# An encoder layer on one Trainium2 core: weight units of the head made one by one, and three output multiplications placed ahead of the last row tiles

## The chip, the cores and the metric

The kernel runs on one core of a Trainium2 chip. Its engines run side by side, each through its own list in order: TensorE (PE, with its weight loads shown as PEld), VectorE (DVE), ScalarE (ACT), GpSimd (POOL, which here issues transfers that add while they store) and SyncE (SP, which issues the plain transfers). They wait for one another through semaphores. The metric is the device time of one execution in microseconds; for the kernel before there are three runs and one profiled execution.

## The reference

One inference step of one layer of a hybrid streaming encoder, over 576 tokens (512 of a new stream, 64 of a running one) with 1024 features, all in fp32:

```
x += 0.5 * SwiGLU_1(RMSNorm(x))              # 1024 -> 2 * 2816 -> 1024
h  = RMSNorm(x); p = h @ w_in                # 7168 columns
y_a = (B * dwconv3(C * V)) @ w_a_out
y_b = swish(LN(dwconv31(GLU(U)) + bias)) @ w_b_out
x += (sigmoid(g_a) * y_a + sigmoid(g_b) * y_b) @ w_out
x += 0.5 * SwiGLU_2(RMSNorm(x))
y  = RMSNorm(x)
```

SwiGLU(v) is (silu(v @ W_gate) * (v @ W_up)) @ W_down. The outputs are y and the new histories of the two convolutions. Only the first SwiGLU (the head of the kernel) and the second one's last part with the final norm (its end) matter here.

## The kernel before

**Layout.** Features lie on the 128 partitions and tokens on the free axis, so an activation is 8 tiles of 128 x 576, and a product takes weights as the stationary operand and two halves of 288 tokens as the moving one.

**fp32 by parts.** Each fp32 operand v is cut into a high part hi (v rounded to the fp32r type, a copy on ACT) and a low part lo = v − hi, and a product is the sum of three matmuls: hi·hi, hi·lo, lo·hi. Weights are cut on the chip, in *units* of up to 512 columns. `Stream` (L195) keeps their order: SP loads raw weights into six buffers (`load`, L224), `add` (L246) makes sums of raws on DVE where a unit needs one, `begin` (L257) casts the high part on ACT, and `end` (L273) makes the low part on DVE. A unit of the kind "dma" has its low part made in another way: ACT also writes −hi, and a POOL transfer adds the raw to it (L267, L268). High and low parts live in tiles of two names, `g` and `u`, taken in turn, so that eight units are in flight at most. A raw buffer is loaded anew when the last unit that reads it is made.

**Lookahead.** `get(n)` (L298) gives unit n to a product. It first calls `lead(n)` (L287), which ends units up to n + ahead − 1, adds the sums of those up to n + ahead + 1 and begins those up to n + ahead. All this is decided while the program is built: the place of a call in the Python code is the place of its instructions in each engine's list.

**The head.** The first SwiGLU has 22 column tiles of gate and up weights, in four groups; the first group has tiles 0 to 4. Tiles 0 and 1 (all but the up weights of tile 1) are multiplied while x is still being loaded. Tiles 0 to 3 are `plain` (L738): a gate product, an up product, then on DVE and ACT `gate` (times the root of the norm, Silu), `hidden` (times up, high part) and `parts` (low part). From tile 4 on, `pair` (L777) computes gate and up of a tile by seven products in place of eight (a form of Strassen's method): sums and differences of weight blocks (s1 to s4) and of activation blocks. The units of the plan (L366 to L368) are, in order: 0 and 1 for up of tile 1, 2 and 3 for gate of tile 2, 4 and 5 for its up, 6 to 9 for tile 3, 10 to 16 for the seven products of tile 4 (10, 14 and 16 are of the kind "dma"; 11, 13 and 15 take the sums s2, s3 and s4, unit 12 takes s1, which is made when unit 10 is added), and from 17 on the down weights of the first group.

**The forms.** The activation side of the seven products needs four forms (`Forms`, L558), one for each pair of feature tiles p and p + 4: `scale` (two ACT operations), `combine` (four DVE operations of 288 columns, two high parts on ACT), `split` (two low parts on DVE). These steps are handed to the first `ffn` as a list, `todo` (L863 to L869), of which `forming` (L772) takes one entry at a time. A plain tile calls it after `gate` and after `parts`.

**The block of units.** After tile 0, `plain` calls `lead` for units 2 and 3, and after tile 1 for units 4 and 5 (L768 to L770), with a lookahead of six (L719).

**The end.** The last group of the second SwiGLU gives the eight row tiles of the output. Rows 3 to 7 (`LATE`) are computed in two passes, first for tokens 0 to 303 and then for tokens 304 to 575 (`LATE_SPANS`). After the first pass the squares of its tokens are summed (`gather`); in the second pass `put` (L1159) makes the root for the first span and returns four steps, each of which multiplies two row tiles by it on DVE and sends them out through SP. They are taken one after each row from row 4 on (L1187 to L1197). Each row of the second pass is taken up by DVE (L1184), squared on ACT, and the square added on DVE; the last square goes to PE by itself, and the root and the four multiplications of the second span close the kernel (L1200).

Of the kernel before, what the change touches and what calls it, by code (L numbers as in the profile page):

```python
# [42 lines left out]
LATE = range(3, KT)  # L43
# [17 lines left out]
AHEAD_UNITS = 6  # L61
# [45 lines left out]
def tile_encoder_step(  # L107
# [87 lines left out]
    class Stream:  # L195
# [88 lines left out]
            self.begin()  # L284
            self.end(low)

        def lead(self, n):  # L287

            self.load_ahead()
            n, total = n + self.ahead, len(self.units)  # L290
            while self.done < min(total, self.begun, n):
                self.end()
            while self.added < min(total, n + 2):
                self.add()
            while self.begun < min(total, n + 1):
                self.begin()
# [7 lines left out]
    ws = Stream(AHEAD_UNITS)  # L304
# [411 lines left out]
    name = ("f1", "u", 1)  # L716
    ps = product(name, xg)
    early[name] = ps
    ws.ahead = AHEAD_UNITS  # L719


    def update(j, ps, R=None):

# [8 lines left out]
    def ffn(f, xg, sums, finish, forms, R=None, todo=()):  # L732
        todo = list(todo)

        rest = []


        def plain(i, hs):  # L738
            nonlocal R
            t, up = ttile(), (f, "u", i)  # L740
            ps = product((f, "g", i), xg, order=IN_TURN if f == "f2" and i == 0 else None)
            got = None if up in early else chunks(up)
            if R is None:
                R = rstd(sums)
            ups = product(up, xg, got=got)
            hs.append(None)
            at = len(hs) - 1

            def gate():
                dve.tensor_tensor(halves(t), ps, halves(R), op=ALU.mult)  # L750
                sca.activation(t, t, AF.Silu)

            def hidden():
                dve.tensor_tensor(halves(t), ups, halves(t), op=ALU.mult)
                hs[at] = high(t)

            def parts():
                hs[at] = hs[at], low(t, hs[at])

            if f == "f2":  # L760
                rest.extend((gate, hidden, parts))
                return
            gate()
            forming()
            hidden()
            parts()
            forming()
            if i < 2:  # L768
                for n in plan[f, "gu"[i], 2]:
                    ws.lead(n)  # L770

        def forming():  # L772
            if todo:
                for step, p in todo.pop(0):
                    step(p)

        def pair(i, hs, last):  # L777
            qu, uu, t, cu = (ttile() for _ in range(4))
            q1, u2, u3, u4 = half(qu, 0), half(qu, 1), half(uu, 0), half(uu, 1)
            q = []  # L780

            def q7():
                dve.tensor_tensor(u3, q[3], u2, op=ALU.add)
                dve.tensor_tensor(half(cu, 1), u3, q[2], op=ALU.subtract)

            def gate():
                dve.tensor_tensor(half(t, 1), q[5], u4, op=ALU.add)
                dve.tensor_tensor(t, t, R, op=ALU.mult)
                sca.activation(t, t, AF.Silu)

            steps = (
                lambda: sca.copy(q1, q[0]),
                lambda: dve.tensor_tensor(u2, q[1], q1, op=ALU.subtract),
                lambda: dve.tensor_tensor(u4, q[2], u2, op=ALU.subtract),
                q7,
                lambda: dve.tensor_tensor(half(t, 0), q[4], q1, op=ALU.add),
                gate,
            )
            for n, xs in enumerate(bs):
                w = ws.get(plan[f, "s", i][n])  # L800
                q.append(bank()[:, :H])
                for k in range(KU):
                    (whi, wlo), (xh, xl) = w, xs[k]
                    for m, (l, r) in enumerate(((whi, xh), (whi, xl), (wlo, xh))):
                        pe.matmul(
                            q[n], l[:, k, :], r, start=k == m == 0, stop=k == KU - 1 and m == 2
                        )
                if n > 0:
                    steps[n - 1]()
                if rest:  # L810
                    rest.pop(0)()

            hs.append(None)
            at = len(hs) - 1

            def up():
                if last:
                    dve.tensor_tensor(t, t, R, op=ALU.mult)
                dve.tensor_tensor(half(cu, 0), q[6], u3, op=ALU.add)

            def hidden():
                dve.tensor_tensor(cu, cu, t, op=ALU.mult)
                hs[at] = high(cu)

            def parts():
                hs[at] = hs[at], low(cu, hs[at])

            rest.extend((up, hidden, parts))

        for g, grp in enumerate(GROUPS):  # L830
            hs = []
            for i in grp:
                if i < PLAIN[f]:
                    plain(i, hs)
                    continue
                if i == PLAIN[f]:
                    bs = forms.operands(xg)
                pair(i, hs, grp[-1] == FT - 1)
            while rest:
                rest.pop(0)()  # L840
            spare.clear()
            if grp[-1] < FT - 1:
                for j, ps in enumerate(both([(f, "d", g, j) for j in range(2)], hs)):
                    update(j, ps, R)
                for j in range(2, KT):
                    update(j, product((f, "d", g, j), hs), R)
            else:
                finish(g, hs)

    def finish1(g, hs):  # L850
        table(AF.Abs_reciprocal_sqrt)
        ps = both([("f1", "d", g, j) for j in range(2)], hs)
        for j in range(KT):
# [2 lines left out]
            nss.square(X[j])  # L856
            nss.add(dve)

    nss, nxg = Sum(), []
    one = forms1  # L860
    ffn(
        "f1", xg, ss, finish1, one, R1,
        (  # L863
            ((lambda _: ws.end(), None), (one.combine, 0), (one.scale, 1)),
            ((one.split, 0), (one.combine, 1), (one.scale, 2)),
            ((one.split, 1), (one.combine, 2), (one.scale, 3)),
            ((one.split, 2), (one.combine, 3)),
            ((one.split, 3),),
        ),  # L869
    )  # L870
    ss, xg = nss, nxg
# [266 lines left out]
    def finish2(g, hs):  # L1138
        fsum = Sum()
        table(AF.Abs_reciprocal_sqrt)  # L1140
        ps = both([("f2", "d", g, j) for j in range(2)], hs)
        for j in range(LATE[0]):
            update(j, ps[j] if j < 2 else product(("f2", "d", g, j), hs))
            fsum.square(X[j])
            fsum.add(dve)
        late = {}
        ydst = y.rearrange("(q a p) t -> q p a t", a=2, p=P)

        ys = {}

        def gained(j, span):

            n = span.stop - span.start
            q, a = j // 2, j % 2
            if a == 0:
                ys[q] = gtile(n=2 * n).rearrange("p (a n) -> p a n", a=2)
            sca.activation(ys[q][:, a, :], X[j][:, span], AF.Copy, scale=par(j, R_NF))

        def put(spans, ys, queues):  # L1159

            i, e = spans[0]
            RF = rstd(fsum, spans)[:, i:e].unsqueeze(1).broadcast_to((P, 2, e - i))

            def rows(q, v):
                dve.tensor_tensor(v, v, RF, op=ALU.mult)
                queues[q % 2].dma_start(ydst[q, :, :, i:e], v)

            return [(lambda q=q, v=v: rows(q, v)) for q, v in ys.items()]

        puts = []  # L1170

        for n, spans in enumerate(LATE_SPANS):
            i, e = spans[0]
            span = slice(i, e)
            fsum.n = LATE[0]
            done = dict(ys)
            for j in LATE:
                if n == 0:
                    late[j] = chunks(("f2", "d", g, j))
                ps = psum2()  # L1180
                for k, (w, kk) in enumerate(late[j]):
                    mm(ps, w, kk, hs[k], k == 0, k == len(hs) - 1, spans)
                xj = X[j][:, span]
                dve.scalar_tensor_tensor(  # L1184
                    xj, ps[:, 0, : e - i], 0.5, xj, op0=ALU.mult, op1=ALU.add
                )
                if n > 0 and j == LATE[1]:  # L1187
                    puts = put(LATE_SPANS[n - 1], done, (nc.sync, nc.sync))
                    fsum.terms = None
                fsum.square(X[j], span=span)  # L1190
                fsum.add(dve)
                if j == LATE[0]:
                    for b in range(LATE[0]):
                        gained(b, span)
                gained(j, span)
                if puts:
                    puts.pop(0)()  # L1197
            if n == 0:
                fsum.gather(span)
        for rows in put(spans, ys, (nc.sync, sca)):  # L1200
            rows()
# [47 lines left out]
```

## Time and profile before

| | |
|---|---|
| runs | 1306.09 us median of 3 (1305.59 to 1307.37) |
| profiled execution | 1304.71 us |
| its span, first to last instruction | 1302.9 us |
| mean granted PE clock | 0.996 |
| busy: PE, DVE, ACT, POOL | 99%, 68%, 59%, 29% of the span |
| PE's waits: for ACT's g tile, for a DMA into g | 3.7 us, 2.2 us |

In the profile nearly every instruction has line 83, that of a helper that records all operations, so operations are told apart by engine, tile names and shapes: `g<-raw` and `u<-raw` are high parts (ACT CAST), scalings by −1 (ACT ACTIVATE `g<-g`) or the adding transfers (POOL DMA) of weight units; `w<-raw,raw` and `w<-w,raw` are sums; `u<-w,u` and `g<-raw,g` low parts; `tmp<-w` and `tmp<-w,tmp` are `combine`, `act<-tmp` high parts and `act<-tmp,act` low parts of activations; `tmp<-mm,r` is a gate and `tmp<-mm,tmp` a product with up. All times are microseconds from the start of the span.

### The profile page before, as it was taken

How to read it: one execution, taken by the hardware profiler on the slowest of the kernel's cores; microseconds unless marked ns; L12 is line 12 of the kernel's file. 1: busy time of each engine (PE TensorE's matmuls, PEld its weight loads, DVE VectorE, ACT ScalarE, POOL GpSimd, SP SyncE). 2: the span in 40 equal slices, each digit the busy share in tenths (PEclk: the TensorE clock that was granted, in tenths of full speed). 3: DMA queues.
4: the chain of work that ended last, by engine and by line, in shares of the span. 5: the costliest groups of instructions: out<-in, count | busy, mean ns of one | idle time of the engine just before them, and what ended most of it. 6: DMA issues, size and time to landing. Idle time of an engine off the chain costs nothing.

```text
span 1302.9 us, 25690 instructions
## 1 busy us (share of the span) xinstructions
PE 1285.8 (99%) x9754; PEld 1283.6 (99%) x9754; DVE 892.3 (68%) x1469; ACT 768.5 (59%) x1362; POOL 380.7 (29%) x481
## 2 busy tenths in 40 slices
PE   9899999999999999999999999999999999999996
PEld 9899999999999999999999999999999999999996
DVE  6748758748945899888885260336967848847955
ACT  7555646645677654555544674457665655654664
POOL 0042332331242554333321322222142141241230
PEclk9999999999999999999999999999999999999998
DMA  7298796796798798878785978776687696796784
GB/s 220 61 175 181 142 196 146 163 194 148 161 185 184 163 214 174 169 168 177 172 169 124 200 160 175 160 163 145 138 169 176 147 195 155 157 210 136 158 176 106
DMA packets 287516, 215.39 MB, mean 165 GB/s; under 512 B 15520, under 2 KB 250016, under 8 KB 287392
## 3 DMA queue, kind: packets, MB, share of 16 engines
q0 software_dynamic: 59184, 97.28, 45.6%
q1 hardware_dynamic: 226336, 115.49, 31.2%
q8 instruction: 77, 1.26, 0.4%
q10 hardware_dynamic: 1872, 0.97, 0.3%
q14 instruction: 47, 0.39, 0.1%
HBM read 113.81 MB, written 2.62 MB: 89 GB/s over the span
## 4 chain that ended last, share of the span: by engine, by line
PE 94%; issue 2%; DVE 1%; ACT 1%; DMA 1%; POOL 0%; DVEq 0%; POOLq 0%; ACTq 0%
PE mm L83 94%; DVE tmp L83 1%; DMA g<-raw 0%; DMA raw<-in_ffn_w_gate_up_dram 0%; DVE g L83 0%; ACT w L83 0%; DMA act<-raw 0%; DVE x L83 0%; ACT act L83 0%; DVE act L83 0%; ACT tmp L83 0%; ACT r L83 0%; ACT L83 0%; DVEq L1239 0%; DVE u L83 0%
## 5 line engine op out<-in xcount | busy, mean ns | idle before, releaser
L83 PE MATMUL mm<-act,u 128*128 128x288 f32 x4686 | 659.9, 293 | 0.0
L83 PEld LDWEIGHTS mm<-act,u 128*128 128x128 f32 x4686 | 630.5, 188 | 0.0
L83 PE MATMUL mm<-act,g 128*128 128x288 f32 x2778 | 401.0, 295 | 5.9 <-ACT g L83 3.7
L83 PEld LDWEIGHTS mm<-act,g 128*128 128x128 f32 x2778 | 379.2, 188 | 6.7 <-ACT g L83 3.9
L83 PE MATMUL mm<-act,act 128*128 128x288 f32 (+2 forms) x2244 | 306.4, 293 | 0.2 <-DMA act<-raw 0.2
L83 PEld LDWEIGHTS mm<-act,act 128*128 128x128 f32 x2244 | 297.3, 188 | 0.5 <-DMA act<-raw 0.5
L83 POOL DMA_DIRECT2D u<-raw x199 | 174.0, 874 | 365.5 <-ACT u L83 295.9
L83 ACT CAST u<-raw 128x512 fp32r<-128x512 f32 (+2 forms) x203 | 116.1, 572 | 157.1 <-PE mm L83 121.7
L83 POOL DMA_DIRECT2D g<-raw x122 | 106.4, 872 | 321.6 <-ACT g L83 245.0
L83 DVE SCALAR_TENSOR_TENSOR w<-g,prm,w 128x606 f32<-128x606 f32 x232 | 179.3, 844 | 1.4 <-ACT w L83 1.4
L83 DVE TENSOR_TENSOR tmp<-mm,tmp 128x288 f32<-128x288 f32 (+1 forms) x239 | 107.7, 459 | 71.7 <-PE mm L83 52.9
L83 POOL DMA_DIRECT2D act<-raw x90 | 78.0, 866 | 199.3 <-ACT act L83 195.6
L83 ACT ACTIVATE u<-u 128x512 fp32r<-128x512 f32 (+2 forms) x199 | 117.9, 593 | 6.3
L83 ACT CAST g<-raw 128x512 fp32r<-128x512 f32 (+2 forms) x126 | 69.0, 547 | 48.2 <-PE mm L83 23.2
L83 ACT CAST act<-tmp 128x576 fp32r<-128x576 f32 x84 | 56.6, 674 | 44.8 <-DVE tmp L83 43.4
L83 ACT CAST u<-w 128x512 fp32r<-128x512 f32 x79 | 48.9, 619 | 57.1 <-DVE w L83 49.8
L83 ACT CAST g<-w 128x512 fp32r<-128x512 f32 x77 | 47.7, 619 | 58.8 <-DVE w L83 51.1
L83 DVE SCALAR_TENSOR_TENSOR tmp<-mm,r 128x576 f32<-128x576 f32 x48 | 36.3, 756 | 64.5 <-PE mm L83 64.5
L83 DVE TENSOR_TENSOR act<-tmp,act 128x576 fp32r<-128x576 f32 x84 | 62.1, 755 | 21.8 <-ACT act L83 20.4
L83 ACT ACTIVATE g<-g 128x512 fp32r<-128x512 f32 (+2 forms) x122 | 69.2, 567 | 3.9
L83 DVE TENSOR_TENSOR w<-raw,raw 128x512 f32<-128x512 f32 x78 | 53.4, 685 | 14.7 <-DMA raw<-in_ffn_w_gate_up_dram 14.7
L83 ACT CAST act<-raw 128x512 fp32r<-128x512 f32 (+3 forms) x94 | 55.6, 592 | 10.4 <-PE mm L83 7.5
(88 smaller groups left out, 804.2 us busy)
## 6 DMA issues: line engine op xcount, KB each, us to landing
raw<-in_ffn_w_gate_up_dram SPq DMA_DIRECT2D x171, 256.0 KB, 3.4
u<-raw POOLq DMA_DIRECT2D x140, 256.0 KB, 4.2
raw<-in_w_in_dram SPq DMA_DIRECT2D x112, 256.0 KB, 3.6
act<-raw POOLq DMA_DIRECT2D x80, 256.0 KB, 4.1
raw<-in_ffn_w_down_dram SPq DMA_DIRECT2D x96, 192.0 KB, 3.7
g<-raw POOLq DMA_DIRECT2D x63, 256.0 KB, 3.9
u<-raw POOLq DMA_DIRECT2D x43, 192.0 KB, 4.5
g<-raw POOLq DMA_DIRECT2D x43, 192.0 KB, 4.5
```

Source lines behind the costliest of these rows:

```text
L83: return self.tc.keep_in_program_order(fn(*args, **kwargs))
```

## The change

In the head, the calls of `lead` at the end of plain tiles 0 and 1 are taken out, and a third call of `forming` is put after `hidden`. The list `todo` has ten entries in place of five. Between the steps of the forms it holds `units(n)`, which is `lead(n)` with a lead of one: it ends the units up to n, adds sums up to n + 2 and begins units up to n + 1. The lookahead stays at two through the plain tiles and becomes six when tile 4 starts. So units 3 to 9 are made one at a time from tile 0's gate to tile 2's gate, unit 10 is begun after tile 2's gate and unit 11 after tile 2's `hidden`, and 12 to 15 are begun after tile 3's gate and the last `split`. Unit 16 is begun, as before, when tile 4 starts.

In the end, `put` for the first span is called at row 3 of the second pass in place of row 4, and no step is taken after row 6: three steps come after rows 3, 4 and 5, and the fourth after row 7, as before.

```
-        def lead(self, n):
+        def lead(self, n, ahead=None):
 
             self.load_ahead()
-            n, total = n + self.ahead, len(self.units)
+            n, total = n + (ahead or self.ahead), len(self.units)
...
     early[name] = ps
-    ws.ahead = AHEAD_UNITS
...
             forming()
             hidden()
+            forming()
             parts()
             forming()
-            if i < 2:
-                for n in plan[f, "gu"[i], 2]:
-                    ws.lead(n)
...
                 if i == PLAIN[f]:
+                    ws.ahead = AHEAD_UNITS
                     bs = forms.operands(xg)
...
+    def units(n):
+
+        ws.lead(n, 1)
+
...
-            ((lambda _: ws.end(), None), (one.combine, 0), (one.scale, 1)),
-            ((one.split, 0), (one.combine, 1), (one.scale, 2)),
-            ((one.split, 1), (one.combine, 2), (one.scale, 3)),
-            ((one.split, 2), (one.combine, 3)),
-            ((one.split, 3),),
+            ((units, 3), (one.combine, 0)),
+            ((one.scale, 1), (units, 4)),
+            ((one.split, 0), (units, 5)),
+            ((one.combine, 1), (units, 6), (units, 7)),
+            ((one.scale, 2),),
+            ((one.split, 1), (one.combine, 2), (one.scale, 3), (units, 8)),
+            ((units, 9), (one.split, 2)),
+            ((units, 10),),
+            ((one.combine, 3),),
+            ((one.split, 3), (units, 14), (units, 14)),
...
-                if n > 0 and j == LATE[1]:
+                if n > 0 and j == LATE[0]:
                     puts = put(LATE_SPANS[n - 1], done, (nc.sync, nc.sync))
...
-                if puts:
+
+                if puts and j != LATE[-2]:
                     puts.pop(0)()
```

## The prediction, made before the result was known

> **What bounds the kernel now.** I read the page first: TensorE (PE) is busy nearly the whole span, so a change can only gain where PE waits, runs at a lower clock, or has finished.
>
> ```profile
> span 1302.9 us, 25690 instructions
> PE 1285.8 (99%) x9754; PEld 1283.6 (99%) x9754; DVE 892.3 (68%) x1469; ACT 768.5 (59%) x1362; POOL 380.7 (29%) x481
> ```
>
> Then the list of waits, for PE alone, and a table of stretches around those waits (columns: length, busy time and count for PE, PEld, DVE, ACT, POOL, then granted PE clock, DMA share, GB/s).
>
> ```profile
> PE mm L83 <- ACT g L83: 3.7, 1, 3.7
> PE mm L83 <- DMA g<-raw: 2.2, 1, 2.2
> ...
> 38.15:41.70 3.55, 0.00 (x0) 0.00 (x0) 1.02 (x3) 3.16 (x6) 0.00 (x0) 1.00 0.01 2
> 41.80:46.90 5.10, 5.10 (x25) 4.93 (x26) 3.61 (x6) 2.53 (x5) 0.00 (x0) 0.67 0.61 168
> 46.80:72.40 25.60, 25.60 (x196) 25.50 (x194) 19.96 (x36) 16.26 (x29) 3.86 (x5) 1.00 0.31 70
> 72.60:74.60 2.00, 0.00 (x0) 0.00 (x0) 1.73 (x4) 1.70 (x5) 1.90 (x3) 1.00 1.06 161
> ```
>
> Two holes, both in the head: one before 41.8 us, whose first 5.1 us afterwards ran at a mean clock of 0.67, and one at 72.5. The timeline says what each waited for.
>
> ```profile
> 31.65 3.32 PE L83 MATMUL mm<-act,g 128*128 128x288 f32 x24
> ...
> 34.81 3.32 PE L83 MATMUL mm<-act,u 128*128 128x288 f32 x24
> 39.79 1.44 ACT L83 ACTIVATE w<-x,gains 128x576 f32<-128x576 f32 x2
> 41.13 0.60 ACT L83 CAST g<-raw 128x512 fp32r<-128x512 f32 x1
> 41.78 5.17 PE L83 MATMUL mm<-act,g 128*128 128x288 f32 x24 [3.65 <-ACT g L83]
> ...
> 62.89 0.69 DVE L83 TENSOR_TENSOR w<-raw,raw 128x512 f32<-128x512 f32 x1
> 65.76 0.86 POOL L83 DMA_DIRECT2D g<-raw  x1 [5.72 <-ACT g L83]
> 68.41 0.62 ACT L83 CAST g<-raw 128x512 fp32r<-128x512 f32 x1
> 69.98 0.86 POOL L83 DMA_DIRECT2D g<-raw  x1 [3.36 <-DVE u L83]
> 74.68 1.60 PE L83 MATMUL mm<-act,g 128*128 128x288 f32 x10 [2.16 <-DMA g<-raw]
> ```
>
> In the plan of weight units (units 0 and 1 are tile 1's up weights, 2 and 3 tile 2's gate, 4 and 5 its up weights, 6 to 9 tile 3, 10 to 16 the seven products of tile 4), the cast at 41.13 is unit 4. It stands in ACT's order behind the scaling of form 2 at 39.79, because the old code makes units 4 to 9 in one block after tile 1's forms. The cast at 68.41 and the DMA at 69.98 are unit 16, the last of tile 4's seven; 62.89 is sum s3, and 65.76 is the DMA of unit 14.
>
> What PE loses: 3.65 of wait, 24 matmuls in 5.17 instead of 3.32 (1.85, the clock), and 2.16: **7.66 us** is all that the head can give, if nothing after it gives it back.
>
> **The head, step by step.** The edit takes the block of units 4 to 9 and the early starts of units 10 to 15 out of the lookahead of six, and puts them one at a time between forms. No matmul, cast, subtraction, sum or transfer is added or dropped; `lead` with a lead of one and the later setting of `ws.ahead` are decided at build time and issue nothing. So only the order on DVE and ACT, and after it on SP and POOL, sets the price. I lay out the new order by hand with these durations (DVE, then ACT, grouped by shape; count, busy and mean ns of one, idle before).
>
> ```profile
> L83 DVE TENSOR_TENSOR act<-tmp,act 128x576 fp32r<-128x576 f32 x12 | 8.5, 753 | 5.4 <-ACT act L83 5.4
> L83 DVE TENSOR_TENSOR tmp<-w,tmp 128x288 f32<-128x288 f32 x8 | 3.6, 455 | 0.1
> L83 DVE TENSOR_TENSOR tmp<-mm,tmp 128x576 f32<-128x576 f32 x4 | 3.0, 753 | 0.8 <-ACT tmp L83 0.8
> L83 DVE TENSOR_TENSOR g<-raw,g 128x512 fp32r<-128x512 f32 x4 | 2.8, 688 | 3.6 <-ACT g L83 3.6
> L83 DVE TENSOR_TENSOR w<-raw,raw 128x512 f32<-128x512 f32 x2 | 1.4, 690 | 1.5 <-DMA raw<-in_ffn_w_gate_up_dram 1.5
> ...
> L83 ACT CAST act<-tmp 128x576 fp32r<-128x576 f32 x12 | 8.1, 671 | 10.3 <-DVE tmp L83 10.1
> L83 ACT ACTIVATE w<-x,gains 128x576 f32<-128x576 f32 x6 | 4.3, 766 | 0.0
> L83 ACT CAST g<-raw 128x512 fp32r<-128x512 f32 x7 | 4.3, 612 | 0.0
> L83 ACT ACTIVATE tmp<-tmp 128x576 f32<-128x576 f32 x4 | 2.7, 687 | 4.3 <-DVE tmp L83 4.3
> ...
> 35.48 2.10 DVE L83 TENSOR_TENSOR act<-tmp,act 128x576 fp32r<-128x576 f32 x3 [1.99 <-ACT act L83]
> ```
>
> Three in 2.10 means that a DVE operation of 576 columns starts 0.70 after the one before it; in the same way I take 0.61 for 512 and 0.40 for 288, and on ACT 0.52 for a cast of 512 (0.55 for the scaling of it that a DMA unit needs), 0.60 for one of 576 and for the Silu, 0.70 for a scaling. A hand-over costs the whole duration and 0.03.
>
> DVE has 20 operations of 576 (4 gates, 4 products, 12 low parts), 16 of 512 and 16 of 288 to do: 14.0 + 9.8 + 6.4 = 30.2 us. What it waited for beside is in the idle column: 5.4 + 0.8 + 3.6 + 1.5 = 11.3. In the new order a unit's subtraction stands in most places where DVE waited for a high part. I find five waits of 0.65 to 0.75 left (unit 7's low part, the low part of tiles 1, 2 and 3, unit 9's) and one of 0.1: 3.7. By that count the chain is 7.6 earlier at its end. Laid out operation by operation it gives, with PE's demand beside it (a unit of 24 matmuls takes 34.81 − 31.65 = 3.16, one of 12 half of that, PE goes on at 38.0 without a hole):
>
> - unit 4: low part ready 34.2, wanted 38.0; unit 5: 37.1 against 41.1; unit 6: 40.0 against 44.3; unit 7: 41.3 against 47.5; unit 8: 47.1 against 50.6; unit 9: 49.8 against 53.8. So the wait of 3.65 goes, and with it the 1.85 of the clock.
> - unit 10: its DMA issued at 50.8, where POOL has nothing else; 3.3 to 4.7 to land (rows below): 54.1 to 55.5, wanted at 57.2.
> - units 11 to 15 stand behind tile 3's gate and the split of form 3 now, in place of ahead of them. Low parts: 11 at 58.3 (wanted 58.8), 12 at 60.2 (60.4), 13 at 60.8 (62.0), 15 at 63.6 (65.4). Almost no spare time.
> - unit 14: DMA issued at 60.7, landing 64.0 to 65.4, wanted at 63.6: **a new wait of 0.4 to 1.8**.
> - unit 16: cast at 62.1 instead of 68.41, that is 6.3 earlier; DMA issued at 63.3, landing 66.6 to 68.0, against 66.7 plus unit 14's wait.
>
> ```profile
> g<-raw POOLq DMA_DIRECT2D x1, 256.0 KB, 3.3
> ...
> g<-raw POOLq DMA_DIRECT2D x1, 256.0 KB, 4.7
> ```
>
> These are the landings of unit 14 (alone) and unit 16 (in the stretch with DMA share 1.06). Their bounds are what I use; no issue of this size around there was quicker than the first. The Trainium skill ("DMA: Bandwidth & Descriptors", Anatomy of one DMA) fits a transfer from the POOL queue with 2.0 us and bytes by 436 GB/s, an estimate of 2.6 us for 256 KB. By it units 14 and 16 would be in time and the whole 7.66 would be won; the trace does not agree with it here, its quickest is 3.3.
>
> **Queues passed.** SP: a raw load starts when the buffer's last unit has its low part, so those of tile 4's four raws go with units 4 to 7, at 34.2, 37.1, 40.0 and 41.3. Sum s1 now stands on DVE ahead of tile 2's gate; it wants the first two at 47.0, some 5 us after the second has landed even if that takes the 4.7 above, so the 1.5 us that DVE waited for it is gone. POOL: only the DMAs of 10, 14 and 16 move, all earlier. The stage after (the down weights) begins its units on ACT right behind unit 16, in the old order; they come earlier by what unit 16 does, and PE, arriving earlier than that, would wait for them. So the head's gain is unit 16's shift: 6.3 by the layout, 7.6 by the count of idle time, never above 7.66. I take **6.5**, near the layout, since each further hand-over can only cost. The list of PE's waits has no other entry as long as these two, the work after the head hangs on PE, and so the shift stays.
>
> **The end.** The first span's root (sum, `rstd`, four multiplications with output) is moved from tile row 4 to tile row 3, and the multiplication of row 6 is left out, so that three are done ahead of rows 6 and 7.
>
> ```profile
> 1282.05 0.47 DVE L83 TENSOR_TENSOR tmp<-acc,tmp 128x304 fp32r<-128x304 f32 x1 [0.51 <-ACT tmp L83]
> 1282.44 0.43 DVE L83 SCALAR_TENSOR_TENSOR x<-mm,x 128x272 f32<-128x272 f32 x1
> ...
> 1284.31 0.44 PE L83 MATMUL mm<-tmp,ones_r 128*128 128x304 f32 x2
> 1284.58 6.83 PE L83 MATMUL mm<-act,act 128*128 128x272 f32 x54
> 1284.87 0.46 DVE L83 TENSOR_SCALAR tmp<-mm 128x304 f32<-128x304 f32 x1
> 1286.87 0.47 DVE L83 SCALAR_TENSOR_TENSOR r<-tmp,r 128x304 f32<-128x304 f32 x1
> 1287.62 0.78 DVE L83 TENSOR_TENSOR g<-g,r 128x608 f32<-128x608 f32 x1
> 1291.67 0.78 DVE L83 TENSOR_TENSOR g<-g,r 128x608 f32<-128x608 f32 x1
> 1292.37 0.43 DVE L83 SCALAR_TENSOR_TENSOR x<-mm,x 128x272 f32<-128x272 f32 x1
> 1293.32 0.73 PE L83 MATMUL mm<-tmp,ones 128*128 128x272 f32 x2 [0.79 <-ACT tmp L83]
> ```
>
> PE's last row is done at 1284.58 + 6.83 = 1291.41, but DVE takes it up at 1292.37, behind the third multiplication. That is 0.96 late. After: the sum's two matmuls stand in front of row 4 and wait for the low part that ends at 1282.52, while row 3 ends at about 1282.0 (18 of 54 matmuls are 2.28, and in the old order row 4 fills that much ahead of 1284.31): PE waits 0.4, and its last row ends at 1291.8. DVE: the root runs from 1282.95 to 1285.4 (2.47 from 1284.87 to the end of the row at 1286.87), the multiplications stand at about 1285.8, 1287.8 and 1289.8 (their old distance), row 6's take-up at 1290.5, its square is summed by 1291.8, and row 7's take-up comes at 1291.85 instead of 1292.37. The fourth multiplication lies in the time in which ACT squares row 7, as before. **Gain 0.5**; bounds: minus 0.4 (the PE wait is paid and DVE wins nothing) and 0.96.
>
> **Sum.** 6.5 + 0.5 = 7.0. The profiled execution took 1304.71 (span 1302.9 and 1.8 around it); 1304.71 − 7.0 = 1297.7. The three runs have a median of 1306.09, 1.4 above it, and this is what is forecast: 1306.09 − 7.0 = **1299.1**.
>
> **Rivals.**
>
> - *All of the head.* The two DMAs land in 3.3, unit 14's wait is 0.4 and is made up by the down weights coming as early: 7.66 + 0.5 = 8.2, so 1297.9. For it: with the loads spread out, the crowd at 72 us (share 1.06) thins. Against it: units 16 to 20 are still issued back to back.
> - *A new hole in tile 4.* Units 11 to 13 have 0.2 to 1.2 us to spare, and they hang on a chain of some twelve hand-overs between ACT and DVE. Each 0.2 later makes 2.4, which is paid in full at unit 11 or 12. Gain 7.0 − 2.4 = 4.6, so 1301.5; with the longer landing of unit 16 (1.3 more) on top 3.3, so 1302.8. Against it: the hand-overs in the rows are what I charged.
> - *The down weights set the pace.* If the DMA rings (share 1.06 at 72.6) and not the buffers hold them, PE comes early and waits there, and only the end's 0.5 stays: 1305.6. Against it: from 46.8 to 72.4 the share is 0.31, so the rings stand empty, waiting for units to be made.
> - *Slower: unit 16 lands later than now.* The place is PE's wait at the seventh product of tile 4; it decides from 74.6 us on, against 66.6 to 68.0 in my layout, and would need a landing of over 11 us where 4.7 is the longest of the two rows. A wait of that length is longer than the 3.65 after which the clock fell, so it costs 1.85 more: at a landing of 75.6, 1.0 + 1.85 − 0.5 = 2.3 slower, 1308.4. The Trainium skill ("TensorE: Matmul & The Clock Gate", Part 1) puts that fall after an idle window of 3.4 us; the trace agrees, its 3.65 wait is followed by 0.67 and the 2.16 one by 1.00 in the tables. By that rule the two short waits that I expect leave the clock alone.
>
> **How the numbers follow.** Forecast (5.5 to 8 us) 0.58; all of the head 0.12; new hole 0.18; down weights 0.07; slower 0.05. A measurement of this kernel can tell about 0.2%, that is 2.6 us, from no change: the first three lie beyond it, so faster 0.88, the fourth is no change, 0.07, and 0.05 for slower. The range leaves out the last two and the worst end of the new hole: 1296.8 (a full head and 1 us of spread between runs) to 1302.8 (a gain of 3.3).
>
> **What would show it.** Right: PE has no wait for ACT's g tile, the clock is 1.00 from 38 to 47 us; unit 4's cast stands near 31.5, and ACT's scalings of the later forms come after it; one or two waits for DMA g of together 0.4 to 3 us between 63 and 69; unit 16's DMA issued near 63; PE full from 70 on; the first multiplication of the end comes about 2 us earlier against PE's last row, and row 7's take-up within 0.1 us of it. Wrong: a wait of PE on DVE or ACT at units 11 to 13, a clock below 1.00 in the head, or a wait in the first down products.

## The result, and the profile after

The changed kernel takes 1300.08 us (1298.89 to 1300.39) against 1306.09: the ratio is 0.9948 with a 95% interval of 0.9934 to 0.9963, so it is faster by 6.0 us. The forecast was 1299.1, with a range of 1296.8 to 1302.8. Most of the mechanism came as foretold; the size of the head's gain did not, and it is the more instructive part.

The first line of the page of the kernel after:

```profile
span 1298.3 us, 25689 instructions
```

The span is 4.6 shorter. Three of the stretches shown for the kernel before (length, busy time and count of PE, PEld, DVE, ACT, POOL, then granted PE clock, DMA share, GB/s):

```profile
38.15:41.70 3.55, 3.55 (x29) 3.55 (x28) 2.85 (x7) 2.91 (x5) 0.00 (x0) 1.00 0.33 92
41.80:46.90 5.10, 5.10 (x41) 5.10 (x40) 4.20 (x9) 2.84 (x5) 0.00 (x0) 1.00 0.30 88
46.80:72.40 25.60, 24.01 (x178) 23.31 (x177) 18.23 (x32) 16.71 (x31) 6.91 (x8) 1.00 0.54 102
```

The hole ahead of 41.8 is gone and the clock is 1.00 throughout, but the third stretch, which was full before, now has 1.6 of idle PE. The timeline of the kernel after shows where:

```profile
28.84 3.33 PE L83 MATMUL mm<-act,u 128*128 128x288 f32 x24
31.59 0.60 ACT L83 CAST g<-raw 128x512 fp32r<-128x512 f32 x1
34.45 1.44 ACT L83 ACTIVATE w<-x,gains 128x576 f32<-128x576 f32 x2
...
61.13 0.86 POOL L83 DMA_DIRECT2D g<-raw  x1 [8.91 <-ACT g L83]
63.60 0.86 POOL L83 DMA_DIRECT2D g<-raw  x1 [1.61 <-DVE u L83]
64.44 1.58 PE L83 MATMUL mm<-act,g 128*128 128x288 f32 x10 [0.40 <-DMA g<-raw]
66.56 0.86 POOL L83 DMA_DIRECT2D u<-raw  x1
70.15 1.06 PE L83 MATMUL mm<-act,u 128*128 128x288 f32 x6 [0.40 <-DMA u<-raw]
72.01 3.76 PE L83 MATMUL mm<-act,u 128*128 128x288 f32 x26 [0.79 <-DMA u<-raw]
75.61 3.39 PE L83 MATMUL mm<-act,g 128*128 128x288 f32 x24
```

The row at 28.84 is unit 1, ahead of everything that the change touches, and the one at 75.61 is a fixed place in the down products behind all of it. The time between the two is called the **head length** from here on; it does not depend on how early an execution got its first loads. 61.13 and 63.60 are the transfers of units 14 and 16. After unit 16 the down weights go on, units 17, 18, 19; 66.56 is unit 19's transfer. PE waits three times: for unit 14 (64.44), unit 17 (70.15) and unit 19 (72.01). The rows of the kernel before for the same places:

```profile
28.49 3.32 PE L83 MATMUL mm<-act,u 128*128 128x288 f32 x24
72.94 0.86 POOL L83 DMA_DIRECT2D u<-raw  x1
80.87 3.32 PE L83 MATMUL mm<-act,g 128*128 128x288 f32 x24
```

Head length: 80.87 − 28.49 = 52.38 before, 75.61 − 28.84 = 46.77 after: **5.6 won**. DVE's groups in the head of the kernel after (count, then busy and mean ns of one, then idle before):

```profile
L83 DVE TENSOR_TENSOR act<-tmp,act 128x576 fp32r<-128x576 f32 x12 | 8.6, 754 | 2.4 <-ACT act L83 2.3
L83 DVE TENSOR_TENSOR u<-raw,u 128x512 fp32r<-128x512 f32 x4 | 2.8, 688 | 1.4 <-ACT u L83 1.4
L83 DVE TENSOR_TENSOR g<-raw,g 128x512 fp32r<-128x512 f32 x4 | 2.7, 684 | 1.0 <-ACT g L83 1.0
L83 DVE TENSOR_TENSOR w<-raw,raw 128x512 f32<-128x512 f32 x2 | 1.4, 684 | 0.0
```

Busy times are those of before within 0.1; the idle column of these groups went from 11.3 to 4.8, and the wait of the sums for their raws is gone. About 1.0 of both figures is one and the same wait, that for unit 2's high part, which stands at the same place in both kernels (the first row is the kernel before, the second the kernel after):

```profile
29.27 0.69 DVE L83 TENSOR_TENSOR g<-raw,g 128x512 fp32r<-128x512 f32 x1 [1.01 <-ACT g L83]
29.61 0.69 DVE L83 TENSOR_TENSOR g<-raw,g 128x512 fp32r<-128x512 f32 x1 [1.01 <-ACT g L83]
```

The end, kernel after:

```profile
1277.85 0.90 PE L83 MATMUL mm<-tmp,ones_r 128*128 128x304 f32 x2
1278.58 9.05 PE L83 MATMUL mm<-act,act 128*128 128x272 f32 x72
1281.55 0.79 DVE L83 TENSOR_TENSOR g<-g,r 128x608 f32<-128x608 f32 x1
1287.67 0.44 DVE L83 SCALAR_TENSOR_TENSOR x<-mm,x 128x272 f32<-128x272 f32 x1
1288.69 0.73 PE L83 MATMUL mm<-tmp,ones 128*128 128x272 f32 x2 [0.23 <-ACT tmp L83]
```

The two sum matmuls take 0.90 where they took 0.44: 0.46 of waiting. PE's last row ends at 1278.58 + 9.05 = 1287.63 and is taken up at 1287.67, 0.04 later instead of 0.96. The root's matmuls come 1.06 after PE's last row, before 1293.32 − 1291.41 = 1.91: 0.85 won on DVE, 0.46 paid on PE, **0.4 won**. The same 0.4 shows from the first matmul of the last pass (tokens 304 to 575) to the last matmul of the program: 13.79 before, 13.40 after. Together 5.6 + 0.4 = 6.0, the measured difference of the medians.

### The profile page after: what moved, and what is told of

Same layout as the page of the kernel before. It is cut to its first block, busy times and chain, and to the rows that moved or that the text cites. A ratio compares the mean times of both kernels' runs of the same rounds, so it can differ in the third digit from the quotient of the medians.

```text
span 1298.3 us, 25689 instructions
## 1 busy us (share of the span) xinstructions
PE 1286.2 (99%) x9754; PEld 1283.6 (99%) x9754; DVE 892.1 (69%) x1469; ACT 768.7 (59%) x1362; POOL 380.7 (29%) x481
## 4 chain that ended last, share of the span: by engine, by line
PE 94%; issue 2%; DVE 2%; DMA 1%; ACT 1%; POOL 0%; DVEq 0%; POOLq 0%; ACTq 0%
PE mm L83 94%; DVE tmp L83 1%; DMA u<-raw 0%; DVE g L83 0%; ACT tmp L83 0%; DMA act<-raw 0%; DMA raw<-in_ffn_w_gate_up_dram 0%; DVE x L83 0%; ACT act L83 0%; DVE acc L83 0%; ACT r L83 0%; DVE act L83 0%; ACT w L83 0%; ACT L83 0%; DVEq L1246 0%
```

## The experiments

The expectations count in part from PE's 160th matmul (4.56 ahead of unit 1's row) and to its 540th (1.6 behind the end of the head length). All kernels but one compute what the kernel before computes, in another order; that one (the first hole filled) adds 24 matmuls, whose result is overwritten.

**The head alone, the end alone.** The changed kernel with the old end:

```
-                if n > 0 and j == LATE[0]:
+                if n > 0 and j == LATE[1]:
...
-                if puts and j != LATE[-2]:
+                if puts:
```

> The head's edit alone, the end as before. Theory (the head gives most): PE's wait for ACT's g tile is gone, unit 16's transfer is issued about 6 us earlier, and the time is 5 to 6 us below the kernel before (about 1300.5). Rival (the gain seen is spread between runs, or the end gives a large part of it): less than 4 us. In the profile the part of PE behind the first down products should again lie 4.5 to 5.5 us earlier than in the profile before.

And the reverse, the kernel before with these two lines as the change has them:

> The end's edit alone, the head as before. Theory: PE waits 0.4 to 0.5 us for the first span's sum ahead of row 4, row 7 is taken up within 0.3 us of PE's last row, and the last matmul comes 0.4 to 0.5 us earlier than before: 1305.6, not to be told from no change by its time. Rival (the wait on PE eats the gain): the last matmul is not earlier, 0 to 0.4 us slower.

Both came as expected. The head alone: 1300.32 (ratio 0.9957, 0.9944 to 0.9969), head length 75.80 − 29.16 = 46.64. The end alone: 1305.64 (0.9995, 0.9986 to 1.0004), head length 52.48. The end's 0.4 is less than run times can tell apart; it rests on the traces: from the first matmul of the last pass to the last matmul, the two profiles of the kernel before and the three runs that keep its end take 13.8 to 13.9, the seven with the new end 13.4. Here is the end alone, where PE's last rows and row 7's take-up stand to each other as above:

```profile
1284.08 9.05 PE L83 MATMUL mm<-act,act 128*128 128x272 f32 x72
1293.16 0.44 DVE L83 SCALAR_TENSOR_TENSOR x<-mm,x 128x272 f32<-128x272 f32 x1
```

1284.08 + 9.05 = 1293.13, taken up at 1293.16. So the two parts add up, and the head is nearly everything.

**Lookahead six again from tile 2.** The changed kernel, with tile 4's units begun earlier:

```
+                if i == 2:
+                    ws.ahead = AHEAD_UNITS
...
-                    ws.ahead = AHEAD_UNITS
```

> The changed kernel, but the lookahead goes back to six at tile 2 and not at tile 4, so units 3 to 8 are still made one by one, while 9 to 15 stand ahead of the gates of tiles 2 and 3, in the old order. Theory A (the first hole comes from the block of units 4 to 9 behind tile 1's forms alone, the order of 10 to 15 gives nothing by itself): no wait before tile 4, unit 14's transfer issued 2 us or more earlier than in the changed kernel and without a wait on it, time equal to the changed kernel or up to 1 us below it (1299.0 to 1300.1). Theory B (the placing of 10 to 15 between the forms is needed): DVE reaches the last split or tile 3's gate too late, PE waits 1 us or more at the second or sixth product of tile 4, time 1 to 3 us above the changed kernel.

Measured: 1299.5 (0.9949, 0.9935 to 0.9963), not to be told from the changed kernel. Its timeline:

```profile
61.19 0.53 PE L83 MATMUL mm<-act,u 128*128 128x288 f32 x2 [0.68 <-DVE act L83]
64.66 0.86 POOL L83 DMA_DIRECT2D g<-raw  x1 [3.84 <-DVE u L83]
75.40 3.32 PE L83 MATMUL mm<-act,g 128*128 128x288 f32 x24
```

Unit 14's wait is gone, but PE now waits 0.68 for the last split at unit 11, and unit 16 goes out 0.9 later than in the changed kernel (64.66 − 29.00 = 35.66 against 34.76 from unit 1's row). The time is that of theory A. The place of the wait is the one that theory B named, with 0.68 in place of 1 or more, and unit 14 goes out 1.3 earlier, not 2. The wait moved; the head length (46.40) hardly did.

**The first hole filled.** The kernel before, with 24 matmuls put into PE's wait ahead of unit 4, so that the clock stays up:

```
         ps = psum2()
+        if name == ("f1", "u", 2):
+            for _ in range(24):
+                pe.matmul(ps[:, 0, :H], ones_r, xs[0][0][:, :H], start=True, stop=True)
```

> The kernel before with 24 matmuls of ones, whose result is overwritten, put on PE between the gate and the up product of tile 2, where PE idles. They fill some 3.1 of the 3.65 us of the wait; the up product can start no earlier. Theory (the lower clock after the wait comes from PE's idleness): the granted clock stays 1.00 from 38 to 47 us, the 24 matmuls from 41.8 on take about 3.5 and not 5.17 us, and the time is 1.6 to 1.85 us below the kernel before. Rival (the clock falls there for another reason): clock and time as before.

Measured: 1307.9 (1.001, 1.0001 to 1.0018). The timeline of this kernel has unit 4's matmuls at 41.95 in 3.60 instead of 5.17, so the clock stayed up:

```profile
41.95 3.60 PE L83 MATMUL mm<-act,g 128*128 128x288 f32 x24 [0.48 <-ACT g L83]
62.71 1.59 PE L83 MATMUL mm<-act,g 128*128 128x288 f32 x10 [1.31 <-DMA g<-raw]
70.08 1.58 PE L83 MATMUL mm<-act,g 128*128 128x288 f32 x10 [0.76 <-DMA g<-raw]
70.17 0.86 POOL L83 DMA_DIRECT2D g<-raw  x1 [3.35 <-DVE u L83]
74.12 1.60 PE L83 MATMUL mm<-act,g 128*128 128x288 f32 x10 [0.59 <-DMA g<-raw]
80.99 3.32 PE L83 MATMUL mm<-act,g 128*128 128x288 f32 x24
```

Head length 80.99 − 28.66 = 52.33, against 52.38. The theory had the clock right and the time wrong: nothing is won. PE, 1.6 ahead, stands 1.31 at unit 10, 0.76 at unit 14, 0.59 at unit 16 and 0.40 at unit 19, and has lost its lead by the end of the head. Unit 16's transfer goes out at 70.17 − 28.66 = 41.51, where it did before (41.49). This shows that the loss of clock cost the kernel before nothing, and that PE's holes do not add up: the head is as long as it takes until its last units are ready. That this kernel is 1.5 slower by its runs does not come from its head. In its profile the stretch from the end of the head to the last pass takes 1200.9, where the eleven other profiles have 1198.6 to 1200.0; why it does is not explained.

**One unit ready earlier.** With the lookahead of six from tile 2, tile 3's last split is put right behind its combine:

```
-            ((one.combine, 3),),
-            ((one.split, 3), (units, 14), (units, 14)),
+            ((one.combine, 3), (one.split, 3)),
+            ((units, 14), (units, 14)),
```

> The changed kernel with lookahead six from tile 2 on, as in the earlier experiment, and the last split right behind the last combine. Theory: the wait of 0.7 us of the second product of tile 4 for that split is gone; unit 16's transfer, issued at 64.7 there, stays within 0.3 us, and so does the point from which PE runs without a wait, since unit 16 and the down weights behind it set it: same time as that experiment (1299.5). Rival (each of PE's waits counts by itself): 0.7 us faster.

And the same with a lookahead of eight at tile 3:

```
+                if 1 < i <= PLAIN[f]:
+                    ws.ahead = 8 if f == "f1" and i == 3 else AHEAD_UNITS
```

> The changed kernel with the units of tile 4 made sooner: lookahead six at tile 2 and eight at tile 3 (units 12 to 17 begun ahead of tile 3's gate), six again from tile 4 on, and the last split of the forms right behind the last combine, ahead of tile 3's units. Theory (what is left of the head's holes is set by when units 14, 16 and 17 are begun on ACT, not by the transfers' speed): unit 14's transfer issued about 2 us and unit 16's 2 us or more earlier than in the changed kernel (61.1 and 63.6), no wait of PE in tile 4, at most 0.6 us in the first down products; PE 1.0 to 1.7 us ahead of the changed kernel behind them; time 1298.4 to 1299.1. Rival (the transfers crowd one another and land as late): the waits move to the down products, gain over the changed kernel under 0.5 us.

The first took 1300.74 (0.9957, 0.9944 to 0.9969), head length 78.14 − 29.18 = 48.96: 2.6 longer than with that lookahead alone (1.2 by the run times), where no difference or a gain of 0.7 was expected, so both readings missed. DVE does the split's low parts ahead of tile 3's units now, and then waits 0.75 for the Silu, a wait that the low parts had filled (row 62.84). Unit 16's transfer goes out 0.9 later (65.78 − 29.18 = 36.60 from unit 1) and lands in 4.6. PE waits 2.09 for it, and then this happens, in the timeline and the stretch table:

```profile
62.84 0.76 DVE L83 TENSOR_TENSOR tmp<-mm,tmp 128x576 f32<-128x576 f32 x1 [0.75 <-ACT tmp L83]
65.78 0.86 POOL L83 DMA_DIRECT2D g<-raw  x1 [3.35 <-DVE u L83]
70.42 1.65 PE L83 MATMUL mm<-act,g 128*128 128x288 f32 x10 [2.09 <-DMA g<-raw]
71.87 6.43 PE L83 MATMUL mm<-act,u 128*128 128x288 f32 x36
```

```profile
70.42:71.87 1.45, 1.45 (x11) 1.45 (x11) 0.00 (x0) 0.01 (x1) 0.92 (x2) 0.99 1.10 165
71.87:73.00 1.13, 1.13 (x7) 1.13 (x6) 0.46 (x1) 0.00 (x0) 0.00 (x0) 0.50 1.10 151
```

The clock falls to 0.50 for some 3.4 us, and 36 matmuls take 6.43 where the kernel before had 4.90: 1.5 more. This time nothing hides it: the transfer that ends the head in the other kernels (unit 19, table below) has landed in time.

The second took 1299.83 (0.9949, 0.9936 to 0.9963), head length 46.46: the waits moved (0.81 at unit 14, 1.03 at unit 19), the time stayed. The theory missed at its first step: unit 16's transfer goes out only 0.6 earlier than in the changed kernel (34.17 from unit 1's row) and unit 14's 0.2 later, so this run does not say what units made 2 us sooner would give.

**Both kernels again.**

> The changed kernel itself, beside the two versions on one chip, and for a second profile of it. Theory: 5.5 to 6.5 us below the kernel before; the waits of PE in the head lie within 0.2 us of the first profile's, and the time between PE's 800th matmul and the last pass is again 1163.9 (0.45 above the profile before), so that what the gain loses there belongs to the kernel. Rival: that stretch differs by 0.4 us or more from the first profile, and so belongs to the single execution.

> The kernel before itself, for a second profile of it. The stretch between PE's 800th matmul and the last pass was 1163.4 us in its profile and 1163.9 in that of the changed kernel. Theory (it belongs to the kernel): 1163.4 again within 0.1. Rival (single executions differ): off by 0.4 or more, like the spread of its runs of 1305.3 to 1308.0.

The changed kernel took 1299.93 (0.9949, 0.9936 to 0.9961), head length 75.44 − 28.57 = 46.87, with the same waits at units 14, 17 and 19 (0.40, 0.47, 0.93): these belong to the kernel, not to one execution. The stretch from PE's 800th matmul to the last pass does not: in the second profile of the kernel before it is 1.0 longer than in the first (1164.3 against 1163.3), where 0.1 was allowed, and in that of the changed kernel 0.2 longer. The kernel before took 1306.62 in one execution, and its timeline is an experiment by itself:

```profile
42.47 5.94 PE L83 MATMUL mm<-act,g 128*128 128x288 f32 x24 [3.40 <-ACT g L83]
75.03 1.61 PE L83 MATMUL mm<-act,g 128*128 128x288 f32 x10 [1.20 <-DMA g<-raw]
78.25 3.70 PE L83 MATMUL mm<-act,u 128*128 128x288 f32 x26 [0.29 <-DMA u<-raw]
81.79 3.32 PE L83 MATMUL mm<-act,g 128*128 128x288 f32 x24
```

The clock cost 0.8 more here than in the first profile (5.94 against 5.17) and the wait at unit 16 is 1.20 instead of 2.16, with 0.29 at unit 19. Head length 81.79 − 29.23 = 52.56. The same code pays the holes in other places and arrives at the same time.

**The block moved, not taken apart.** The kernel before, with its block of units 4 to 9 placed ahead of a step of the forms:

```
-            forming()
             if i < 2:
                 for n in plan[f, "gu"[i], 2]:
                     ws.lead(n)
+            forming()
```

> The kernel before with one edit: the block of lead calls of tiles 0 and 1 stands ahead of their second forms step in place of behind it; still one block, lookahead six. Theory (making units one by one matters, since each then fills a wait of DVE for a high part): PE's first hole of 3.65 us is gone or under 0.5, but the chain of DVE and ACT keeps its waits for high parts and for the raws of the first sum, so unit 16's transfer is issued only 1 to 3.5 us earlier than before against PE's 160th matmul (46.05), not 6.7 as in the changed kernel, PE waits more at tile 4, and the time lies 1 to 3.5 us below the kernel before (1303 to 1305.4). Rival (the block only had to come earlier): unit 16 5 us or more earlier, time within 1 us of the changed kernel.

Measured: 1303.89 (0.9981, 0.9971 to 0.999), head length 49.69, as the theory had it: unit 16's transfer goes out 2.5 earlier. That is 2.7 of the 5.6. The hole at unit 4 is gone, PE's next wait is 0.81 at unit 6, and the clock stays at 1.00. What the one-by-one order adds is the other 2.9: DVE's wait for the activations' high parts in this kernel is as long as in the kernel before (5.4), and only that for the units' went, from 3.6 to 1.0.

```profile
L83 DVE TENSOR_TENSOR act<-tmp,act 128x576 fp32r<-128x576 f32 x12 | 8.7, 753 | 5.4 <-ACT act L83 5.4
L83 DVE TENSOR_TENSOR g<-raw,g 128x512 fp32r<-128x512 f32 x4 | 2.7, 687 | 1.0 <-ACT g L83 1.0
```

**A buffer of its own for the last raw of tile 4.** By now one quantity stood out. From unit 1's row, in us:

| kernel | unit 16 issued | unit 19 issued | its landing takes | unit 19 landed | head length |
|---|---|---|---|---|---|
| before | 41.49 | 44.45 | 4.35 | 48.80 | 52.38 |
| before, second profile | 41.69 | 44.64 | 4.33 | 48.97 | 52.56 |
| end alone | 41.65 | 44.61 | 4.29 | 48.89 | 52.48 |
| first hole filled | 41.51 | 44.48 | 4.26 | 48.74 | 52.33 |
| block moved | 38.95 | 41.91 | 4.26 | 46.16 | 49.69 |
| after | 34.76 | 37.72 | 5.40 | 43.13 | 46.77 |
| after, second profile | 34.76 | 37.71 | 5.62 | 43.33 | 46.87 |
| head alone | 34.77 | 37.73 | 5.31 | 43.04 | 46.64 |
| lookahead six | 35.66 | 38.61 | 4.20 | 42.81 | 46.40 |
| split moved, lookahead eight | 34.17 | 39.21 | 3.67 | 42.88 | 46.46 |
| split moved | 36.60 | 39.56 | 4.30 | 43.86 | 48.96 |
| own buffer (below) | 34.74 | 37.70 | 4.84 | 42.54 | 46.06 |

Head length less landing of unit 19 is 3.52 to 3.64 in every row, the 26 matmuls that stand behind it; only the kernel that lost its clock there has 5.10. The kernel before has no wait at unit 19 in its first profile, but PE comes to it only 0.1 to 0.2 after it landed. The transfer's landing is in the list of DMA issues, first for the kernel before, then for the one after:

```profile
u<-raw POOLq DMA_DIRECT2D x1, 192.0 KB, 4.4
```

```profile
u<-raw POOLq DMA_DIRECT2D x1, 192.0 KB, 5.4
```

So unit 19 is issued 6.73 earlier in the changed kernel and lands 1.05 slower: 5.68, the head's gain (5.6). In the changed kernel the raw load of unit 21 goes out together with the transfer of unit 17; in the kernels where unit 17 lands within 4.7 it goes 0.9 to 2.3 ahead of it, and with lookahead eight, where unit 17 takes 5.4, 0.7 behind it. With a buffer of its own for the last raw, that load no longer waits, and goes out some 5 us earlier:

```
-                t = wraw.tile([P, KU, P], F32, tag="raw", name=nm("raw"))[:, :k, :]
+                if len(self.loaded) == 13:
+                    t = wtile(n=KU * P).rearrange("p (k n) -> p k n", n=P)
+                else:
+                    t = wraw.tile([P, KU, P], F32, tag="raw", name=nm("raw"))[:, :k, :]
```

> The changed kernel with the last raw of tile 4 in a buffer of its own (one of the activation side), so that no raw load waits for unit 14's transfer: the load for unit 21, issued together with unit 17's transfer in the changed kernel, goes some 4 us earlier. Theory (that load slows the transfers of units 17 and 19 from 4.0 to 4.6 to 5.3 to 5.6 us): they land in 3.9 to 4.7, PE's two waits in the first down products (0.4 and 0.8 to 0.9) fall to 0.3 or less together, and the stretch from PE's 160th to its 540th matmul is 52.0 to 52.4 instead of 52.8 to 53.0 us. Rival (the five transfers crowd one another by themselves): landings of 5.3 or more again, waits as before.

Measured: 1299.29 (0.9945, 0.9932 to 0.9959), not to be told from the changed kernel by its time. Its timeline:

```profile
29.64 3.32 PE L83 MATMUL mm<-act,u 128*128 128x288 f32 x24
67.34 0.86 POOL L83 DMA_DIRECT2D u<-raw  x1
75.70 3.28 PE L83 MATMUL mm<-act,g 128*128 128x288 f32 x24
```

Unit 19 is issued at 37.70 as in the changed kernel, lands in 4.84 instead of 5.40, and the head length is 46.06, 0.7 shorter. The landing followed the load, and the head followed the landing, but only half of the way back to 4.3, so the theory holds in part: units 17 and 19 land in 4.9 and 4.8 where 3.9 to 4.7 were expected, PE's wait at unit 17 is gone, but that at unit 19 is still 0.85. The stretch from PE's 160th to its 540th matmul is 52.2, as expected. The rest stays open. Another load is still issued among these transfers; and in all kernels in which unit 17 takes 4.9 or more, unit 14's transfer goes out 1.7 to 2.5 ahead of unit 16's, in all others 4.2 to 4.7. No run here moves that distance alone.

## Why the prediction was right, and where it was off

**The first hole and its cause: right.** Unit 4's cast stands at 31.59 (foretold 31.5), ahead of the scaling of the later forms at 34.45; PE has no wait for ACT's g tile, and the clock is 1.00 from 38 to 47. No unit from 4 to 13 makes PE wait: the rival of a new hole at units 11 to 13 fell, although they had the little spare time given (with lookahead six, unit 11 was hit, for 0.68).

**Unit 14: right.** Its transfer goes out at 61.13 (60.7), lands 3.3 later, and PE waits 0.40, the lower bound of 0.4 to 1.8.

**Unit 16: right.** Cast and transfer come 41.49 − 34.76 = 6.73 earlier, between the layout's 6.3 and the 7.6 by the count of idle time, near the 6.5 taken. It landed at 63.60 + 3.8 = 67.4, when PE came to it. The five waits of DVE that the prediction found left are there, 0.66 to 0.80 each and 3.7 together. Its count of 7.6 was 1.0 too high all the same: the 11.3 held the wait for unit 2 (the row at 29.27), which stays. 11.3 − 1.0 − 3.7 = 6.6 is near the measured 6.73.

**The step that failed in size** is the one behind it: the down weights "come earlier by what unit 16 does", and so "the head's gain is unit 16's shift". They are issued earlier by just that (44.45 − 37.72 = 6.73), but they take longer to land. The prediction priced landings for units 14 and 16 alone (3.3 to 4.7) and so let those of the down weights stay as they were; units 17 and 19 took 4.6 and 4.4 before and take 5.5 and 5.4 now. PE waits 0.40 and 0.79 for them, and the term is 5.6 instead of 6.5. (The prediction says of such waits once that PE would have them, and at its end that they would show it wrong.) I had followed when SP's loads of tile 4's raws start, but not which transfers the loads behind them then meet; the kernel with its own buffer gives half of the 1.05 to such a load. By the fit of the Trainium skill ("DMA: Bandwidth & Descriptors", Anatomy of one DMA), 2.0 us and bytes by 436 GB/s, a transfer of 192 KB from the POOL queue takes an estimated 2.45 us. The trace does not agree: the quickest of that size in any kernel here took 2.99.

**What was right for a wrong reason** is the ceiling. The 7.66 was made of 3.65, 1.85 and 2.16, as if each could be won. The filled hole shows that these are not terms of a sum: 3.65 and 1.85 were on PE alone, and of the 1.6 that it regained nothing was left at the end of the head. The ceiling held because the chain of DVE and ACT, which sets unit 16, happened to move by less. With PE's holes as the only guide, filling the first hole would have been forecast as a gain of 1.85, and it gave none.

**Rivals.** "All of the head" fell with the landings. "The down weights set the pace" was the right place with the wrong price: they do set it, and took 1.1 of the 6.73, not all. "Slower" needed unit 16 later than before; it came 6.7 earlier.

**The end: right.** PE's wait was 0.46 (foretold 0.4), row 7 is taken up 0.04 after PE's last row (0.05), and the first multiplication comes 6.1 ahead of it instead of 3.8. Gain 0.4 for 0.5.

**The sum.** 5.6 + 0.4 = 6.0 for 7.0, and the median came 1.0 above the forecast. The spans alone could not have shown this: the second profiles of the kernel before and the one after have 1304.8 and 1297.5. The difference is 7.3 here and 4.6 in the first pair, while the head length gives 52.56 − 46.87 = 5.7 and 5.6. The rest lies in the first loads (unit 1's row is at 28.49 in one profile of the kernel before and at 29.23 in the other) and in the long middle of the program, from the end of the head to the last pass: 1199.0 and 1200.0 before, 1200.0 and 1199.3 after.

## What to carry to other kernels

Where PE stands idle several times in a row, do not add up its holes: find the last thing that it waits for in that stage, and follow that thing's issue and landing from a fixed row ahead of the edit; what it moves is the gain, and filling an earlier hole only makes the later ones longer. When work is pulled forward, ask of each transfer what else is in flight at its new time, since a landing taken from the old place is a price of the old place. And measure a gain of a few us between two rows that frame the edit, when spans of the same code differ by a third of it.

## What the hardware did that I had not expected

**The clock can fall after a hole of 2.1 us, and the same hole can cost different amounts.** The kernel with the split moved lost the clock after 2.09 of wait; the kernel before kept it after 2.16. (The prediction read this from the row 72.60:74.60, which is the wait itself; the first row below lies behind it.) In the kernel before, the first hole cost 5.17 − 3.32 = 1.85 in one profile and 5.94 − 3.39 = 2.6 in the other; in the end alone, whose head is the same, it cost 6.13 − 3.39 = 2.7. When the fall comes differs too. In the kernel with the split moved, matmuls run at 1.00 for 1.4 after the hole (the row 70.42 above), and in the first profile of the kernel before for 1.3. In its second profile the clock falls 1.3 ahead of the end of the hole (in the second row below it is low throughout; PE starts at 42.47). The low spell lasts 3.4 in the first two and 6.8, twice that, in the third and in the end alone.

```profile
76.13:78.00 1.87, 1.87 (x17) 1.87 (x16) 0.46 (x1) 0.00 (x0) 0.00 (x0) 1.00 1.14 194
42.00:43.00 1.00, 0.53 (x2) 0.53 (x3) 0.55 (x1) 1.00 (x3) 0.00 (x0) 0.50 0.00 0
```

The Trainium skill ("TensorE: Matmul & The Clock Gate", Part 1) speaks of a free-running window of 3.4 us. The lengths of the spells agree, and windows of that phase would explain why a hole counts or not by where it falls; no run here tries it. Its condition of a whole idle window does not agree: 2.09 was enough here. That short waits leave the clock alone holds for all waits of 0.3 to 1.5 in the heads of these kernels; a wait of about 2 can go either way.

**Matmuls of one kind run at one of several paces.** The 18 matmuls of a row in the first down products take 2.50, 2.53 or 2.58 at a clock of 1.00, and one pace holds for some two hundred matmuls: in the changed kernel 2.58 in one profile and 2.50 in the other.

```profile
78.83 2.58 PE L83 MATMUL mm<-act,u 128*128 128x288 f32 x18
```

```profile
78.56 2.50 PE L83 MATMUL mm<-act,u 128*128 128x288 f32 x18
```

In the kernel with the first hole filled the pace changes where PE starts again after a wait (24 matmuls take 3.32 ahead of it and 3.28 behind), in the changed kernel also at 103.0 without one. It would be part of the spread between executions; what chooses it was not tried.
